# Second mixer of a two-layer fp32 network: TensorE order written out by hand, the sink as a column behind the keys, softmax scaling on GpSimd

## The chip, the cores and the metric

The program runs on one core of a Trainium2 chip. The metric is the device time of one execution in microseconds (us), the median over runs; times of the kernel before are shown below. Engines: TensorE (PE, matrix products), VectorE (DVE), ScalarE (ACT), GpSimd (POOL), SyncE (SP, which only issues DMA transfers here).

## The reference, cut to what matters

The network has two layers over 512 tokens of width 1024, all in fp32: mixer, feed-forward with a short convolution, gated embedding; the first layer's mixer is `mixer_ab`, the second layer's is `mixer_c`, which the change rewrites. It is attention in a sliding window with 16 query heads of 64 (4 key heads), blocks of 128 queries against 256 keys, and one learned "sink" per head: a logit that takes part in the softmax and has no value.

```python
q, k, v = jnp.split(h @ w_in, [1024, 1280], axis=-1)
q, k = rmsnorm(q heads, q_norm), rmsnorm(k heads, k_norm)
...
logits = einsum('bqhgd,bkhd->bhgqk', qn, kn) * 0.125 + bias
logits = where(mask, logits, -inf)
m = maximum(max(logits, -1), sink)
e = exp(logits - m)
w = e / (sum(e, -1) + exp(sink - m))
o = einsum('bhgqk,bkhd->bqhgd', w, vn)
...
h = h + o @ w_out
```

## The kernel before, in words

**Projections.** A product with fp32 accuracy is made of three: every operand is split into a high and a low half (fp32r), and `mm3` (L185 to L187) issues hi·hi, lo·hi, hi·lo. A projection tile (128 output rows x 512 tokens, buffer `psfm`) has 8 slices of the inner dimension, so 24 matmuls of 128x512, in two halves of 12. One half uses one weight chunk of 512 columns: `weights` (L157 to L172) loads it by DMA, ScalarE casts the high half (`whi`, L170), VectorE subtracts (`wlo`, L171). `fm_steps` yields after each half, and `fm` runs one to its end.

**The second mixer**, `mixer_c`. First come the keys' two projection tiles (a first stretch that starts as soon as input tiles are there), the values (`tm`, L218 to L220, buffer `pstm`), the token norms (`norm`, and `columns`, L270, buffer `psc`). Queries come in 8 tiles `jt` of two heads each. `project(jt)` is a projection with its scaling (`y`, L727) and its square (`sqc`, L729); `normed` sums squares per head with one fp32 matmul (`pn`, L735), ScalarE takes Ln and Exp (through the helper at L71), VectorE makes `qn` (L739).

The attention of a tile has two units of two blocks each (n0 = 0 and 2), 16 units in all:

- `scores(jt, n0)`: four fp32 matmuls on 64-row halves (`pl`, L765; 128 keys for block 0, else 256), four reductions on VectorE that add the bias and take the maximum with the sink (L771), the negated maximum `nm` and the sink's term `es` (L775, L776), four Exp on ScalarE in place in `lg`, which leave the sums in `dn`, one Exp of `es`, then `dn` plus `es` and its reciprocal (L783, L784), and four scalings of `lg` by it on VectorE (L788).
- `values(jt, n0)`: 6 or 8 transposes (`pt`, L800), copies out of PSUM (`wt`, ScalarE for one head, VectorE for the other, L806, L809), 6 or 8 matmuls with the values (`poc`, L817, on 64-column halves); after the second unit the tile is split for the output projection (L178, L179).

At the end `fill()` runs `embed`: the embedding projection of the next stage, 8 tiles of 6 matmuls (`pspp`), which need nothing of the mixer.

**What sets the order.** The program names the work of a tile in the order scores, projection, values of two units before; the Tile scheduler then orders every engine's instructions itself, so TensorE's queue may change from one kind of work to another after any matmul. Each engine executes its queue in order.

Of the kernel before, what the change touches and what calls it, by code (L numbers as in the profile page):

```python
# [23 lines left out]
NT = T // P  # L24
# [11 lines left out]
V_KN = V_QN + 1  # L36
# [9 lines left out]
PLAN = "hdsdhdsdhdsdhdhdshs"  # L46
LAST = "hdsdhdsdhdsdhdhshds"
SW_ORDER = [g * 4 + i for gg in (0, 2) for i in range(4) for g in (gg, gg + 1)]


class Kern:
# [649 lines left out]
    def mixer_c(self, st, bias, fill):  # L701
        nc, A = self.nc, self.A
        xs = st["xs"]
        W = A["w_c"]
        with ExitStack() as ctx:
            kp = self.pool("c_keep", 1, ctx=ctx)
            tp = self.pool("c_tmp", 2, ctx=ctx)
            first = self.lead([W[8], W[9]], st)
            pss = [t[:, a, :] for t in (self.zpair("pstm"), self.zpair("pstm")) for a in range(2)]
            tok = self.tm(A["w_cv"], xs, 256, pss)  # L710
            for _ in range(LEAD[0]):
                next(tok)
            self.norm(st, "hg")
            rstd = st["rstd"]
            for _ in range(LEAD[1]):
                next(tok)
            self.columns(st, "hg")
            sink = kp.tile([P, 16], F32, name="sink")
            nc.gpsimd.dma_start(out=sink, in_=A["sinks"].partition_broadcast(P))
            gq = kp.tile([P, 1], F32, name="gq")  # L720
            nc.vector.tensor_scalar(out=gq, in0=self.v(V_QN), scalar1=0.125, scalar2=None, op0=ALU.mult)

            def project(wi):

                ps = first.pop(0) if first else self.fm(W[wi], xs)
# [4 lines left out]
                return y, sq  # L730

# [9 lines left out]

            kn = [project(8 + i) for i in range(2)]
            kn = [normed(*x, self.v(V_KN), "kn", 2) for x in kn]
            vt = []
            for _ in tok:
                pass
            for i in range(NT):
                t = kp.tile([P, 256], F32, tag="vt", name="vt", bufs=4)
                nc.scalar.activation(t, pss[i][:, 0:256], AF.Identity, scale=st["rcol"][:, i:i + 1])
                vt.append(t)  # L750
            os_, qs, pos, pend = [], {}, {}, []

            def scores(jt, n0):

                q, kt = qs[jt], kn[jt // 4]
                wid = [128 if n == 0 else 256 for n in (n0, n0 + 1)]
                lg = []
                mx, nm, dn, es = [tp.tile([P, 4], F32, tag=t, name=t, bufs=4) for t in ("mx", "nm", "dn", "es")]
                pls = self.zpair("pl").rearrange("p a (i k) -> p a i k", i=2)
# [6 lines left out]
                for a in range(2):  # L766
                    hd = 2 * jt + a
                    l = tp.tile([P, 2, 256], F32, tag="lg", name="lg", bufs=6)
                    for i in range(2):
                        nk = wid[i]  # L770
# [3 lines left out]
                    lg.append(l)  # L774
                nc.vector.tensor_scalar(out=nm, in0=mx, scalar1=-1.0, scalar2=None, op0=ALU.mult)  # L775
                nc.vector.tensor_tensor(out=es.rearrange("p (a i) -> p a i", a=2), in0=nm.rearrange("p (a i) -> p a i", a=2),  # L776
                                        in1=sink[:, 2 * jt:2 * jt + 2].unsqueeze(2).broadcast_to([P, 2, 2]), op=ALU.add)
# [12 lines left out]

            def values(jt, n0, wid, lg):
                if n0 == 0:
                    pos[jt] = self.bank("poc", "hg")
                po = pos[jt]
                wts = []
                pts = self.zpair("pt").rearrange("p a (i k) -> p a i k", i=2)
                for a in range(2):
                    for i in range(2):
                        for b in range(wid[i] // P):
                            nc.tensor.transpose(out=pts[:, a, i, b * P:(b + 1) * P], in_=lg[a][:, i, b * P:(b + 1) * P], identity=self.ident)  # L800
                for a in range(2):
# [8 lines left out]
                    wts.append(wt)  # L810
                for i in range(2):
                    n = n0 + i
# [9 lines left out]

            two = [project(jt) for jt in range(2)]
            for jt in range(2):
                qs[jt] = normed(*two[jt], gq, "qn", 3)
            for jt in range(8):
                for n0 in (0, 2):
                    pend.append(scores(jt, n0))
                    if jt + 2 < 8:
                        if n0 == 0:  # L830
                            nxt = project(jt + 2)
                        else:
                            qs[jt + 2] = normed(*nxt, gq, "qn", 3)
                    if len(pend) > 2:
                        values(*pend.pop(0))
            for x in pend:
                values(*x)
            fill()
            return os_
# [46 lines left out]
    def embed(self, L, pp, pr):  # L886
# [3 lines left out]
        for c0 in range(2):  # L890
            for d0, hi, lo in self.weights(A[f"w_pp{L}"][c0], 1024):
                for j in range(2):
# [5 lines left out]
                    nc.scalar.copy(out=o, in_=ps)  # L898
                    pr.append(o)

    def ple(self, L, st, nxt, pp, pr):
        nc, A = self.nc, self.A
        xs = st["xs"]
        with ExitStack() as ctx:
            tp = self.pool(f"p_tmp{L}", 2, ctx=ctx)
            if pr:
                first = self.lead(A[f"w_pg{L}"][0:2], st)
            else:
                first = []
                self.embed(L, pp, pr)  # L910
            self.norm(st)
# [141 lines left out]
```

## Time and profile before

| what | value |
|---|---|
| median of 3 runs | 1327.49 us (1326.45 to 1328.64) |
| the profiled execution's own time | 1326.3 us |
| its span in the trace | 1324.5 us |
| TensorE busy | 1309.1 us, 99% of the span |
| VectorE, ScalarE, GpSimd busy | 65%, 52%, 1% |
| mean granted TensorE clock | 0.999 of full speed |

The profile shows one execution. The span runs from the first to the last instruction that the trace holds, and the execution's own time is 1.8 us longer. Busy shares are means over the whole program; the second mixer is about a tenth of it. In a row of the timeline, consecutive instructions of one form stand together with their count: one fp32 matmul (`pl`, `poc`, `pn`) is recorded as two, so that `pl ... x6` is three matmuls; a matmul of split halves (`psfm`) and a transpose are recorded as one. Durations of consecutive rows overlap by some tenths, because matmuls are pipelined; what a piece costs is the distance between the starts of two rows.

### The profile page before, as it was taken

How to read it: one execution, taken by the hardware profiler on the slowest of the kernel's cores; microseconds unless marked ns; L12 is line 12 of the kernel's file. 1: busy time of each engine (PE TensorE's matmuls, PEld its weight loads, DVE VectorE, ACT ScalarE, POOL GpSimd, SP SyncE). 2: the span in 40 equal slices, each digit the busy share in tenths (PEclk: the TensorE clock that was granted, in tenths of full speed). 3: DMA queues.
4: the chain of work that ended last, by engine and by line, in shares of the span. 5: the costliest groups of instructions: out<-in, count | busy, mean ns of one | idle time of the engine just before them, and what ended most of it. 6: DMA issues, size and time to landing. Idle time of an engine off the chain costs nothing.

```text
span 1324.5 us, 16856 instructions
## 1 busy us (share of the span) xinstructions
PE 1309.1 (99%) x6162; PEld 1055.2 (80%) x6162; DVE 863.1 (65%) x1609; ACT 684.0 (52%) x1224; POOL 18.7 (1%) x108
## 2 busy tenths in 40 slices
PE   9999999999999999999999999999999999999998
PEld 7787767788888888888888866678888888888887
DVE  6567876766677347776558387755777536776555
ACT  6566876845345224444465466654544324455341
POOL 2000000000000000000000000000000000000000
PEclk9999999999999999999999999999999999999999
DMA  6321211134553333323333211122332333332332
GB/s 208 108 64 49 59 39 47 48 98 116 90 142 98 106 102 101 99 91 94 107 112 91 85 48 32 33 82 94 102 102 89 94 107 96 96 96 88 90 109 80
DMA packets 38821, 118.96 MB, mean 90 GB/s; under 512 B 4433, under 2 KB 10881, under 8 KB 38737
## 3 DMA queue, kind: packets, MB, share of 16 engines
q1 hardware_dynamic: 38032, 116.41, 29.5%
q0 software_dynamic: 560, 1.45, 0.5%
q8 instruction: 48, 0.79, 0.2%
q14 instruction: 37, 0.30, 0.1%
q10 hardware_dynamic: 144, 0.02, 0.0%
HBM read 115.37 MB, written 2.49 MB: 89 GB/s over the span
## 4 chain that ended last, share of the span: by engine, by line
PE 93%; DVE 4%; ACT 2%; issue 1%; DMA 0%; SPq 0%; DVEq 0%; ACTq 0%
PE psfm L185 25%; PE psfm L187 25%; PE psfm L186 25%; PE pl L765 2%; PE poc L817 2%; PE pstm L220 1%; PE pstm L218 1%; PE pstm L219 1%; PE pt L800 1%; PE poa L593 1%; ACT sl L71 1%; PE psz L576 1%; PE pn L735 1%; PE psl L443 1%; PE pspp L185 1%; PE pspp L187 1%
## 5 line engine op out<-in xcount | busy, mean ns | idle before, releaser
L185 PE MATMUL psfm<-xhi,whi 128*128 128x512 f32 (+1 forms) x1200 | 470.8, 393 | 1.3 <-ACT xhi L235 1.3
L170 ACT CAST whi<-wraw 128x512 fp32r<-128x512 f32 (+1 forms) x428 | 260.0, 613 | 406.2 <-PE psfm L186 319.9
L186 PE MATMUL psfm<-xlo,whi 128*128 128x512 f32 (+1 forms) x1200 | 467.0, 389 | 0.8 <-DVE xlo L236 0.7
L187 PE MATMUL psfm<-xhi,wlo 128*128 128x512 f32 (+1 forms) x1200 | 467.5, 390 | 0.1
L171 DVE TENSOR_TENSOR wlo<-wraw,whi 128x512 fp32r<-128x512 f32 (+1 forms) x428 | 287.9, 677 | 170.4 <-ACT whi L170 149.5
L185 PEld LDWEIGHTS psfm<-xhi,whi 128*128 128x128 f32 x1200 | 226.0, 188 | 49.3 <-issue 2.0
L186 PEld LDWEIGHTS psfm<-xlo,whi 128*128 128x128 f32 x1200 | 225.8, 188 | 48.8 <-DVE xlo L236 2.3
L187 PEld LDWEIGHTS psfm<-xhi,wlo 128*128 128x128 f32 x1200 | 225.5, 188 | 47.6 <-issue 1.3
L185 PE MATMUL psfm<-ghi,whi 128*128 128x512 f32 x352 | 136.9, 389 | 0.0
L186 PE MATMUL psfm<-glo,whi 128*128 128x512 f32 x352 | 136.9, 389 | 0.0
L187 PE MATMUL psfm<-ghi,wlo 128*128 128x512 f32 x352 | 136.9, 389 | 0.0
L858 DVE TENSOR_TENSOR u<-psfm,rstd 128x512 f32<-128x512 f32 x88 | 60.7, 691 | 64.0 <-PE psfm L187 60.4
L861 ACT ACTIVATE cy<-u,vec 128x512 f32<-128x512 f32 x88 | 71.7, 817 | 43.8 <-DVE u L858 43.8
L862 DVE SCALAR_TENSOR_TENSOR cy<-u,vec,cy 128x512 f32<-128x512 f32 x88 | 66.1, 752 | 39.0 <-ACT cy L861 38.9
L185 PEld LDWEIGHTS psfm<-ghi,whi 128*128 128x128 f32 x352 | 66.1, 188 | 13.7
L187 PEld LDWEIGHTS psfm<-ghi,wlo 128*128 128x128 f32 x352 | 66.1, 188 | 13.7
L186 PEld LDWEIGHTS psfm<-glo,whi 128*128 128x128 f32 x352 | 66.1, 188 | 13.7
L291 DVE TENSOR_TENSOR h<-h,psfm 128x512 f32<-128x512 f32 x48 | 33.0, 688 | 57.3 <-PE psfm L187 57.3
L863 DVE SCALAR_TENSOR_TENSOR cy<-u,vec,cy 128x512 f32<-128x512 f32 x88 | 65.9, 751 | 2.7
L875 ACT CAST ghi<-cy 128x512 fp32r<-128x512 f32 x44 | 27.4, 623 | 49.4 <-DVE cy L872 49.4
L236 DVE SCALAR_TENSOR_TENSOR xlo<-h,gains,xhi 128x512 fp32r<-128x512 f32 x48 | 36.5, 761 | 7.0 <-ACT xhi L235 6.6
L235 ACT ACTIVATE xhi<-h,gains 128x512 fp32r<-128x512 f32 x48 | 34.6, 724 | 11.0 <-DVE h L291 6.8
(216 smaller groups left out, 1303.3 us busy)
## 6 DMA issues: line engine op xcount, KB each, us to landing
wraw<-w_up SPq DMA_DIRECT2D x88, 512.0 KB, 3.5
wraw<-w_dn SPq DMA_DIRECT2D x32, 512.0 KB, 3.5
wraw<-w_ab SPq DMA_DIRECT2D x18, 512.0 KB, 3.5
wraw<-w_pg SPq DMA_DIRECT2D x16, 512.0 KB, 3.5
wraw<-w_dn SPq DMA_DIRECT2D x32, 192.0 KB, 2.3
wraw<-w_c SPq DMA_DIRECT2D x10, 512.0 KB, 3.4
wraw<-w_abo SPq DMA_DIRECT2D x8, 512.0 KB, 3.6
wraw<-w_co SPq DMA_DIRECT2D x8, 512.0 KB, 3.5
```

The costliest lines, as they stand in the source:

```text
L170: nc.scalar.copy(out=hi[:, :d1 - d0], in_=r)
L171: nc.vector.tensor_tensor(out=lo[:, :d1 - d0], in0=r, in1=hi[:, :d1 - d0], op=ALU.subtract)
L185: t.matmul(ps, w[0], x[0], start=first, stop=False)
L186: t.matmul(ps, w[0], x[1], start=False, stop=False)
L187: t.matmul(ps, w[1], x[0], start=False, stop=last)
L235: nc.scalar.activation(hi, h, AF.Identity, scale=g)
L236: nc.vector.scalar_tensor_tensor(out=lo, in0=h, scalar=g, in1=hi, op0=ALU.mult, op1=ALU.subtract)
L291: self.nc.vector.tensor_tensor(out=self.h[m], in0=self.h[m], in1=ps, op=ALU.add)
L858: nc.vector.tensor_tensor(out=u[:, 2:], in0=ps, in1=rstd, op=ALU.mult)
L861: nc.scalar.activation(y, u[:, 2:], AF.Identity, scale=w[2], bias=w[3])
L862: nc.vector.scalar_tensor_tensor(out=y, in0=u[:, 1:T + 1], scalar=w[1], in1=y, op0=ALU.mult, op1=ALU.add)
L863: nc.vector.scalar_tensor_tensor(out=y, in0=u[:, 0:T], scalar=w[0], in1=y, op0=ALU.mult, op1=ALU.add)
```

## The change

1. In `mixer_c`, TensorE's instructions keep the order in which the program names them (`tc.manual_schedule` for that engine); the other engines are still ordered by the scheduler. The order is a table: before the scores of unit u stand DENSE[u] steps of `dense()`, where a step is half a projection (12 matmuls) for units 0 to 11 and a tile of the embedding projection (6 matmuls) after them. `embed` becomes a generator for that.
2. The transposes leave `values` and become `turned`. Behind the scores of unit u stand the value products of unit u-3, then (in even units) `pn` of the next query tile, then the transposes of unit u-2. From unit 14 on only one scored unit is kept back, from unit 16 on none, so that unit 14 turns two units.
3. The sink becomes column 256 of `lg`: GpSimd copies its negative there (L753 of the changed kernel), the reduction works on negated logits with a minimum, so that it gives `nm` itself, and the Exp runs over 129 or 257 columns, so that `dn` holds the sink's term. `mx`, `es`, its Exp and two small VectorE operations per unit go, the negation too.
4. The 64 scalings by `dn` go from VectorE to GpSimd (L771 of the changed kernel).

The matmuls are the same 5771 instructions in both programs.

```diff
+DENSE = [1] * 12 + [1, 2, 2, 1, 1, 1]
...
-                    l = tp.tile([P, 2, 256], F32, tag="lg", name="lg", bufs=6)
+                    nc.gpsimd.tensor_copy(out=lg[a][:, :, 256:257], in_=nsink[:, hd:hd + 1, :].broadcast_to([P, 2, 1]))
...
-                            out=l[:, i, :nk], in0=pls[:, a, i, :nk], in1=bias[:, hd, 256 - nk:256], scale=1.0,
-                            scalar=sink[:, hd:hd + 1], op0=ALU.add, op1=ALU.max, accum_out=mx[:, 2 * a + i:2 * a + i + 1])
+                            out=lg[a][:, i, 256 - nk:256], in0=pls[:, a, i, :nk], in1=bias[:, hd, 256 - nk:256], scale=-1.0,
+                            scalar=nsink[:, hd, :], op0=ALU.add, op1=ALU.min, accum_out=nm[:, c:c + 1])
-                nc.vector.tensor_scalar(out=nm, in0=mx, scalar1=-1.0, scalar2=None, op0=ALU.mult)
-                nc.vector.tensor_tensor(out=es.rearrange("p (a i) -> p a i", a=2), ...
...
-                        self.act(SET_EL, lg[a][:, i, :wid[i]], lg[a][:, i, :wid[i]], AF.Exp, bias=nm[:, c:c + 1], accum_out=dn[:, c:c + 1])
-                self.act(SET_EL, es, es, AF.Exp)
-                nc.vector.tensor_tensor(out=dn, in0=dn, in1=es, op=ALU.add)
+                        l = lg[a][:, i, 256 - wid[i]:257]
+                        self.act(SET_EL, l, l, AF.Exp, scale=-1.0, bias=nm[:, c:c + 1], accum_out=dn[:, c:c + 1])
                 nc.vector.reciprocal(out=dn, in_=dn)
...
-                        nc.vector.tensor_scalar(out=lg[a][:, i, :wid[i]], in0=lg[a][:, i, :wid[i]], scalar1=dn[:, c:c + 1], scalar2=None, op0=ALU.mult)
+                        nc.gpsimd.tensor_scalar(out=l, in0=l, scalar1=dn[:, c:c + 1], scalar2=None, op0=ALU.mult)
...
+                for u in range(18):
+                    for _ in range(DENSE[u]):
+                        next(d)
+                    if u < 16:
+                        scored.append(scores(u // 2, u % 2 * 2))
+                    for x in keyed:
+                        values(*x)
+                    keyed = []
+                    if u % 2 == 0 and u // 2 + 1 < 8:
+                        qs[u // 2 + 1] = normed(*got[u // 2 + 1], gq, "qn", 3)
+                    while len(scored) > (u < 14) + (u < 16):
+                        keyed.append(turned(*scored.pop(0)))
```

TensorE before, one tile `jt` in the middle of the mixer; a row is a line, an operation and a tile form, with a count where it repeats. Some single `psfm` rows stand between the pieces, and the other 21 or so of the tile follow in a row.

```order
L800 MATMUL pt<-cst,lg 128x128 x6
L765 MATMUL pl<-kn,qn 128x256
L817 MATMUL poc<-wt,vt 64x128
L765 MATMUL pl<-kn,qn 128x256 x2
L817 MATMUL poc<-wt,vt 64x128 x5
L765 MATMUL pl<-kn,qn 128x256
L735 MATMUL pn<-sqc,cst 128x512
L800 MATMUL pt<-cst,lg 128x128 x8
L185 MATMUL psfm<-xhi,whi 128x512
L765 MATMUL pl<-kn,qn 128x128 x2
```

```order
L765 MATMUL pl<-kn,qn 128x256
L817 MATMUL poc<-wt,vt 64x128
L765 MATMUL pl<-kn,qn 128x256
L186 MATMUL psfm<-xlo,whi 128x512
L817 MATMUL poc<-wt,vt 64x128 x7
L187 MATMUL psfm<-xhi,wlo 128x512
```

The two fences are one stretch, the second follows the first. The four score products of a unit stand in two or three pieces, with single value products between them.

TensorE after the change, in the same place: first an even unit (n0 = 0), with the last matmul of its 12 ahead of it, then an odd one.

```order
L189 MATMUL psfm<-xhi,wlo 128x512
L750 MATMUL pl<-kn,qn 128x128 x2
L750 MATMUL pl<-kn,qn 128x256 x2
L804 MATMUL poc<-wt,vt 64x128 x8
L729 MATMUL pn<-sqc,cst 128x512
L781 MATMUL pt<-cst,lg 128x128 x6
L187 MATMUL psfm<-xhi,whi 128x512
```

```order
L750 MATMUL pl<-kn,qn 128x256 x4
L804 MATMUL poc<-wt,vt 64x128 x6
L781 MATMUL pt<-cst,lg 128x128 x8
L187 MATMUL psfm<-xhi,whi 128x512
```

Score products, value products and transposes of a unit now stand each in one piece, and 12 `psfm` stand together between two units: a tile has 9 runs of one kind where it had 15.

GpSimd after the change, two units in the middle of the mixer, an odd one's scalings first (`dn` is the reciprocal sum, `nsink` the negated sink). Before, its queue held nothing in the mixer but the load of the sinks.

```order
L771 TENSOR_SCALAR lg<-lg,dn 128x256 x4
L753 COPY lg<-nsink 128x2
L771 TENSOR_SCALAR lg<-lg,dn 128x128
L771 TENSOR_SCALAR lg<-lg,dn 128x256
L771 TENSOR_SCALAR lg<-lg,dn 128x128
L771 TENSOR_SCALAR lg<-lg,dn 128x256
L753 COPY lg<-nsink 128x2 x3
```

One of an odd unit's two copies stands behind the four scalings of the unit before it, so that its third and fourth Exp wait for those.

## Rows read from the trace of the kernel before

**Rows 1.** Page, parts 1 and 2: busy times, and the granted clock in 40 slices.

```profile
PE 1309.1 (99%) x6162; PEld 1055.2 (80%) x6162; DVE 863.1 (65%) x1609; ACT 684.0 (52%) x1224; POOL 18.7 (1%) x108
...
PEclk9999999999999999999999999999999999999999
```

**Rows 2.** Timeline of PE, ends of the stretch: start us, us, instruction, [idle before].

```profile
736.98 0.95 PE L270 MATMUL psc<-cst,rstd 128*128 128x1 f32 x8
...
757.92 1.12 PE L735 MATMUL pn<-sqc,cst 128*128 128x512 f32 x2 [0.65 <-ACT sqc L729]
758.50 0.79 PE L185 MATMUL psfm<-xhi,whi 128*128 128x512 f32 x1
...
871.95 0.40 PE L185 MATMUL psfm<-xhi,whi 128*128 128x512 f32 x1
```

**Rows 3.** Timeline of PE, one query tile.

```profile
803.80 0.82 PE L800 MATMUL pt<-cst,lg 128*128 128x128 f32 x6
804.55 0.70 PE L765 MATMUL pl<-kn,qn 64*128 64x256 f32 x2
805.17 0.43 PE L817 MATMUL poc<-wt,vt 128*64 128x128 f32 x2
805.54 0.70 PE L765 MATMUL pl<-kn,qn 64*128 64x256 f32 x4
806.17 0.87 PE L817 MATMUL poc<-wt,vt 128*64 128x128 f32 x10
806.97 0.70 PE L765 MATMUL pl<-kn,qn 64*128 64x256 f32 x2
807.59 1.12 PE L735 MATMUL pn<-sqc,cst 128*128 128x512 f32 x2
808.56 1.04 PE L800 MATMUL pt<-cst,lg 128*128 128x128 f32 x8
809.35 0.47 PE L185 MATMUL psfm<-xhi,whi 128*128 128x512 f32 x1
809.75 0.92 PE L765 MATMUL pl<-kn,qn 64*128 64x128 f32 x6
810.63 0.43 PE L817 MATMUL poc<-wt,vt 128*64 128x128 f32 x2
...
812.05 1.09 PE L817 MATMUL poc<-wt,vt 128*64 128x128 f32 x14
813.07 0.50 PE L187 MATMUL psfm<-xhi,wlo 128*128 128x512 f32 x1
813.41 0.39 PE L185 MATMUL psfm<-xhi,whi 128*128 128x512 f32 x1
...
818.20 0.82 PE L800 MATMUL pt<-cst,lg 128*128 128x128 f32 x6
```

**Rows 4.** Timeline of PE, two units whose score products stand in one piece.

```profile
791.39 1.13 PE L765 MATMUL pl<-kn,qn 64*128 64x256 f32 x6
792.45 0.44 PE L817 MATMUL poc<-wt,vt 128*64 128x128 f32 x4
...
795.48 0.93 PE L765 MATMUL pl<-kn,qn 64*128 64x128 f32 x8
796.33 0.50 PE L185 MATMUL psfm<-xhi,whi 128*128 128x512 f32 x1
```

**Rows 5.** Windows: us, busy of PE, PEld, DVE, ACT, POOL, PEclk, DMA share, GB/s.

```profile
800.00:820.00 20.00, 20.00 (x121) 14.03 (x117) 14.66 (x53) 13.10 (x42) 0.00 (x0) 1.00 0.10 29
```

**Rows 6.** Groups by form, 775 to 872: count | busy us, mean ns | idle before.

```profile
L71 ACT ACTIVATE lg<-lg,nm 128x256 f32<-128x256 f32 x40 | 19.8, 497 | 0.0
L788 DVE TENSOR_SCALAR lg<-lg,dn 128x256 f32<-128x256 f32 x42 | 12.8, 348 | 0.0
```

**Rows 7.** Groups by form on POOL, whole span.

```profile
L312 POOL CAST hgm<-mf 128x384 uint8<-128x384 f32 x4 | 3.6, 932 | 0.7 <-DMA mf<-hgm 0.7
L148 POOL CAST cstr<-cstt 128x384 fp32r<-128x384 f32 x1 | 0.5, 510 | 0.6 <-DMA cstt<-cst 0.6
```

More of the change, by code (lines that the diff above doesn't have):

```diff
@@ L707, in mixer_c, with project @@
             tp = self.pool("c_tmp", 2, ctx=ctx)
[L708 to L717, printed above, removed]
             sink = kp.tile([P, 16], F32, name="sink")
             nc.gpsimd.dma_start(out=sink, in_=A["sinks"].partition_broadcast(P))
+            nsink = kp.tile([P, 16, 1], F32, name="nsink")
+            nc.vector.tensor_scalar(out=nsink[:, :, 0], in0=sink, scalar1=-1.0, scalar2=None, op0=ALU.mult)
             gq = kp.tile([P, 1], F32, name="gq")
             nc.vector.tensor_scalar(out=gq, in0=self.v(V_QN), scalar1=0.125, scalar2=None, op0=ALU.mult)
-            def project(wi):
-                ps = first.pop(0) if first else self.fm(W[wi], xs)
+            def project(wi, out):
+                ps = first.pop(0) if first else (yield from self.fm_steps(W[wi], xs))
                 y = tp.tile([P, T], F32, tag="y", name="y")
@@ L729, in project @@
                 nc.scalar.activation(sq, y, AF.Square)
-                return y, sq
+                out[wi] = (y, sq)
             def normed(y, sq, gain, tag, bufs):
@@ L740, in normed @@
                 return o
[L742 to L751, printed above, removed]
+            os_, qs, pos, got, kn, vt = [], {}, {}, {}, [None, None], []
             def scores(jt, n0):
@@ L756, in scores @@
                 wid = [128 if n == 0 else 256 for n in (n0, n0 + 1)]
-                lg = []
-                mx, nm, dn, es = [tp.tile([P, 4], F32, tag=t, name=t, bufs=4) for t in ("mx", "nm", "dn", "es")]
+                lg = [tp.tile([P, 2, 257], F32, tag="lg", name="lg", bufs=6) for _ in range(2)]
+                nm, dn = [tp.tile([P, 4], F32, tag=t, name=t, bufs=4) for t in ("nm", "dn")]
                 pls = self.zpair("pl").rearrange("p a (i k) -> p a i k", i=2)
@@ L767, in scores @@
                     hd = 2 * jt + a
[L768 removed]
+                    nc.gpsimd.tensor_copy(out=lg[a][:, :, 256:257], in_=nsink[:, hd:hd + 1, :].broadcast_to([P, 2, 1]))
+                for a in range(2):
+                    hd = 2 * jt + a
                     for i in range(2):
[L770 removed]
+                        nk, c = wid[i], 2 * a + i
                         nc.vector.tensor_tensor_reduce(
[L772 to L777 removed]
+                            out=lg[a][:, i, 256 - nk:256], in0=pls[:, a, i, :nk], in1=bias[:, hd, 256 - nk:256], scale=-1.0,
+                            scalar=nsink[:, hd, :], op0=ALU.add, op1=ALU.min, accum_out=nm[:, c:c + 1])
                 for a in range(2):
@@ L810, in values @@
                     wts.append(wt)
+                return jt, n0, wid, wts
+            def values(jt, n0, wid, wts):
+                if n0 == 0:
+                    pos[jt] = self.bank("poc", "hg")
+                po = pos[jt]
                 for i in range(2):
@@ L821, in values @@
                     os_.append(self.split_tile(self.xa, po))
[L823 to L835, printed above, removed]
@@ L836, in mixer_c, with dense @@
-            for x in pend:
-                values(*x)
-            fill()
+            def dense():
+                for jt in range(2, 8):
+                    steps = project(jt, got)
+                    next(steps)
+                    yield
+                    for _ in steps:
+                        pass
+                    yield
+                yield from fill()
+            first = self.lead([W[8], W[9]], st)
+            with tc.manual_schedule(engines={mybir.EngineType.PE}):
+                pss = [t[:, a, :] for t in (self.zpair("pstm"), self.zpair("pstm")) for a in range(2)]
+                tok = self.tm(A["w_cv"], xs, 256, pss)
+                for _ in range(LEAD[0]):
+                    next(tok)
+                self.norm(st, "hg")
+                rstd = st["rstd"]
+                for _ in range(LEAD[1]):
+                    next(tok)
+                self.columns(st, "hg")
+                for i in range(2):
+                    for _ in project(8 + i, got):
+                        pass
+                for _ in tok:
+                    pass
+                for i in range(NT):
+                    t = kp.tile([P, 256], F32, tag="vt", name="vt", bufs=4)
+                    nc.scalar.activation(t, pss[i][:, 0:256], AF.Identity, scale=st["rcol"][:, i:i + 1])
+                    vt.append(t)
+                for _ in project(0, got):
+                    pass
+                for i in range(2):
+                    kn[i] = normed(*got[8 + i], self.v(V_KN), "kn", 2)
+                for _ in project(1, got):
+                    pass
+                qs[0] = normed(*got[0], gq, "qn", 3)
+                d = dense()
+                scored, keyed = [], []
+                for u in range(18):
[10 more added lines that the diff above has]
+                        keyed.append(turned(*scored.pop(0)))
+                for x in keyed:
+                    values(*x)
+                for _ in d:
+                    pass
@@ L909, in ple @@
                 first = []
-                self.embed(L, pp, pr)
+                for _ in self.embed(L, pp, pr):
+                    pass
             self.norm(st)
```

11 lines of the change are left out of this document (5 added, 6 removed).

## The prediction

> **What bounds the kernel now.** I read the busy times first: TensorE is busy for 99% of the span, at a granted clock of nine tenths or more in each of the 40 slices [rows 1]. So time can leave only where TensorE does its work in less time, and the matmuls stay the same. What can shrink is what a matmul costs in its surroundings, and for that I went to TensorE's timeline in the mixer. The stretch that the change rewrites runs from the `psc` products at 736.98 to the first product of the output projection at 871.95: 134.97 us [rows 2]. The waits in it are small, 0.65 us ahead of the first `pn` being the largest [rows 2]. One query tile from transposes to transposes takes 818.20 − 803.80 = 14.40 us [rows 3].
>
> In that tile the reader is to see three prices, all as distances between starts:
> - 22 `psfm` from 813.07 to 818.20 take 5.13: the first .34, the other 21 take 4.79, so .228 each. A `psfm` alone between two other kinds costs .40 (809.35 to 809.75) [rows 3].
> - A lone score product (804.55, "x2") costs .62, and two together (805.54, "x4") .63: two products on the two 64-row halves run side by side, and one that stands alone pays for both [rows 3].
> - Value products likewise: one costs .37 (805.17), five .80 (806.17), seven 1.02 (812.05) [rows 3]. I take .80 for six (three pairs) and 1.02 for eight (four pairs).
>
> **The order of TensorE: the term that carries the sum.** Prices of the new pieces: 12 `psfm` are .40 + 11 × .228 = 2.91; 6 are 1.54. Four score products in one piece are .85 for an even unit (795.48 to 796.33) and 1.06 for an odd one (791.39 to 792.45, where three products fill the two pairs) [rows 4]. `pn` is .97, eight transposes .79 (808.56) [rows 3]; for six I take 6/8 of it, .59. So
> - even unit: 2.91 + .85 + 1.02 + .97 + .59 = 6.34;
> - odd unit: 2.91 + 1.06 + .80 + .79 = 5.56;
> - a tile 11.90 where it was 14.40, so 2.50 less.
>
> It can be checked from the other side. The odd unit's score products (804.55, 805.54, 806.97) cost .62 + .63 + .62 and the even one's .88 (809.75) and once more .62, in a piece like that at 804.55 which is left out [rows 3]; now 1.06 and .85: 1.46 less. Value products cost .37 + .80 + .37 + 1.02 [rows 3], now 1.82: .74 less. The rest is `psfm` that stood alone.
>
> The stretch, then: the opening (keys, values, first two query tiles) was 758.50 − 736.98 = 21.52; less the .65 of waiting, less one `pn` that moves back into unit 0 (.85, since part of it overlapped), plus .40 for one more change of kind: 20.4. Units 0 to 3: no value products before unit 3 and no transposes before unit 2, so 6.34 − 1.02 − .59 = 4.73, 5.56 − .80 − .79 = 3.97, 6.34 − 1.02 = 5.32, and 5.56, together 19.6. Units 4 to 11, four tiles, 47.6. Units 12 to 17 have one or two embedding tiles (1.54 or 2.91) in place of the projection: unit 12 is 4.97 and 13 is 5.56 by the same sums; 14, without `pn` but with two units' transposes, 2.91 + .85 + 1.02 + 1.38 = 6.16; 15, with 14 value products and six transposes, 5.01; the last two 1.54 + .80 + .79 and 1.54 + 1.02. Together 27.4. Sum 115.0.
>
> **The tail.** Nothing follows the last scored unit but embedding tiles, so here a wait may show. Between its score products and its transposes TensorE has 1.06 + 1.82 + .59 + 1.54 + .80 = 5.8 us of work. It needs a reduction, four Exp of .497 [rows 6] plus their sums, a reciprocal and four scalings: by these some 6 to 7. I take 1.0, with 0 and 3 as ends. Stretch 116.0, so 134.97 − 116.0 = **19.0 us** less.
>
> **Scaling on GpSimd.** Before, GpSimd does nothing in the mixer [rows 5], so no row has this operation there. Nearest rows: casts of 128x384 in .510 and .932 [rows 7]; by width a 128x256 lies between .34 and .62, and with no credit for the width .93 is the upper end. I take .45, as an fp32 result is nearer to the cheaper cast. 64 of them are 29 us of an engine that is otherwise idle; 8 per tile are 3.6 of 11.9. What hides them is the distance from a unit's scores to its transposes, two units or about 12 us, of which the chain up to the scaled `lg` needs 6 to 7. So their cost is nothing outside the tail, and a fall below nothing is excluded there, because TensorE is already without waits. Without that cover each unit would wait up to 1.8 us (4 × .45), 29 in all.
> A library load stands ahead of the first scaling, and no row shows its like. GpSimd is free from before 737, and the first transposes come some 33 us later (20.4 + 4.73 + 3.97 + 4.3), so it costs nothing up to about 30 us. The Trainium skill ("GPSIMD Engine Reference", section "2.1 Instruction dispatch") puts the first call of freshly loaded code at about 6 us; by that figure the sum stays as it is, and no row here shows it.
>
> **What this takes from the other engines.** VectorE was busy 14.66 of 20 us [rows 5], that is 10.6 per tile; eight scalings of at most .348 [rows 6] leave it, so 7.8 of the new 11.9. ScalarE, 13.10 of 20 [rows 5], has 9.4 per tile, less the Exp of `es`. Both fit, ScalarE with 2.5 us to spare. The small operations that the sink column removes (`nm`, `es`, its Exp, the addition) and the column that each Exp gains lie beside TensorE's work: nothing, covered by that same reserve; without it they would be worth about a microsecond per tile. The 32 copies of the sink go to GpSimd, between scalings. An odd unit's second copy stands behind four scalings of the unit before, and two of its Exp wait for it: those scalings end some 6.5 us after their score products, the Exp's turn comes some 9 after (one unit, then 3), so 2.5 us are left.
>
> **The sum.** The profiled execution took 1326.3; less 19.0 it is 1307.3. The median of the runs shown is 1.2 higher, 1327.49, and less 19.0 gives **1308.5**.
>
> **Rivals.**
> 1. *VectorE and ScalarE come late although their sums fit.* TensorE now follows a fixed order: when a reduction is late, the score products of the next unit stand still, and everything behind them too, where before another `psfm` could stand in the queue. For it: ScalarE's 9.4 of 11.9; VectorE and GpSimd work on the same buffers at once, which no row shows. If each of the three VectorE operations per tile with two inputs outside PSUM (`wlo` twice, `qn`) is held up by one scaling, that is 3 × .45 = 1.35 per tile, and if all of it reaches TensorE, 8 × 1.35 = 10.8: **1319.3**. The Trainium skill ("SBUF — State Buffer", "Who interferes with whom") states such a lock between a VectorE operation with two inputs in SBUF and a GpSimd operation that reads SBUF; no row here shows the two at work side by side. Against it: VectorE would still be at 9.2 of 11.9, and a unit has more than 5 us between the release of its scores and their reuse. Chance .12.
> 2. *The changes of kind were not what cost.* If single `psfm` cost the same in their new place, and only pairing returns: the lone score products of a tile (three, .31 each) and the lone value products (two, .18) give 1.3, so 8 × 1.3 = 10.4 less, **1317.1**. Against it: the same piece stands whole and split in the rows, .85 against 1.50. Chance .06.
> 3. *GpSimd becomes the bound* (slower). Its queue from the first scaling, about 29 us into the stretch, is 64 scalings of s, 32 copies of about .3 (an estimate, below the cheaper cast), and 4 us for the last transposes and values. The stretch is 29 + 64 s + 9.6 + 4: it decides from s = 1.15 on (116), and is as long as before at s = 1.45. At 2.0 it is 170.6, so 35.6 more: **1363**. For it: only two forms of GpSimd's work are in the trace, and twice the dearer of them is 1.9. Against it: both are below 1.15 at greater width. Chance .06.
> 4. *Waits in the tail and at the start eat the gain*, within .2% of before. Nothing points to 17 us of them. Chance .03.
>
> **How the numbers follow.** My forecast, chance .73, is 1305 (no wait in the tail, 2 us of overlaps that the distances hide) to 1313 (3 us in the tail, a few tenths of waiting in each unit). The likeliest is 1308.5. With a chance of .73 the range must take in another case; I take it to 1318, which covers rival 2 and most of rival 1, and leave out rivals 3 and 4 and the rest of 1. About .2%, 2.7 us, is what a measurement of this kernel can tell from no change. Faster by more: forecast, rivals 1 and 2, .91. Same: .03. Slower: rival 3, .06.
>
> **What would show it.** On the changed kernel's timeline of TensorE a tile in the middle should take 12.0 us within .3, in 9 runs, with score products of .85 and 1.06 and 12 `psfm` of 2.9; from `psc` to the output projection some 116 us; the wait ahead of the last transposes 0 to 3 us; scalings on GpSimd below 1 us each, VectorE about 8 of 12. Idle time of TensorE ahead of transposes released by GpSimd would speak for rival 3, ahead of score products by VectorE for rival 1, and full business with a longer tile for rival 2. The forecast is wrong if the stretch saves less than 12 us.

## The result, and the profile after

The changed kernel takes **1312.32 us** (median of 4 runs, 1311.30 to 1312.59) against 1327.28 before: a ratio of 0.9884, with a 95% interval from 0.9872 to 0.9897. That is 15.0 us less, where 19.0 were forecast; the forecast of 1308.5 was too low by 3.8, and the range from 1305 to 1318 holds the time. The profiled execution took 1311.3 us, with a span of 1309.5, so it stands 15.0 below the profiled execution of before too.

The page's busy times come first. They answer to [rows 1]:

```profile
PE 1293.6 (99%) x6162; PEld 1050.0 (80%) x6162; DVE 842.1 (64%) x1498; ACT 680.9 (52%) x1208; POOL 84.4 (6%) x204
```

TensorE executes the same 6162 recorded instructions in 15.5 us less of busy time. It is still busy for 99% of the span. GpSimd has 66 us more to do.

TensorE's timeline at the borders of the forecast's parts (start us, us, instruction, [idle before]), which answers to [rows 2]:

```profile
736.86 0.95 PE L272 MATMUL psc<-cst,rstd 128*128 128x1 f32 x8
...
750.77 1.12 PE L729 MATMUL pn<-sqc,cst 128*128 128x512 f32 x2 [0.78 <-ACT sqc L73]
752.67 0.50 PE L187 MATMUL psfm<-xhi,whi 128*128 128x512 f32 x1 [0.78 <-ACT sqc L73]
...
759.19 0.51 PE L187 MATMUL psfm<-xhi,whi 128*128 128x512 f32 x1
...
778.89 0.47 PE L187 MATMUL psfm<-xhi,whi 128*128 128x512 f32 x1
...
826.86 0.47 PE L187 MATMUL pspp<-whi 128*128 128x512 f32 x1
...
856.82 0.50 PE L187 MATMUL psfm<-xhi,whi 128*128 128x512 f32 x1
```

From the first to the last row the stretch is 119.96 us, where it was 134.97: the whole gain lies here. Its parts beside the forecast:

| part | forecast | measured | rows |
|---|---|---|---|
| opening, to the first projection of unit 0 | 20.4 | 22.3 | 736.86 to 759.19 |
| units 0 to 3 | 19.6 | 19.7 | to 778.89 |
| units 4 to 11, four tiles | 47.6 | 48.0 | to 826.86 |
| units 12 to 17 and the tail's wait | 27.4 + 1.0 | 30.0 | to 856.82 |
| sum | 116.0 | 120.0 | |

So the 4.0 us that are missing lie in the opening (1.9) and the tail (1.6), hardly in the tiles. One tile in the middle, on the same timeline; it answers to [rows 3]:

```profile
800.17 1.13 PE L750 MATMUL pl<-kn,qn 64*128 64x256 f32 x8
801.23 0.88 PE L804 MATMUL poc<-wt,vt 128*64 128x128 f32 x12
802.04 1.09 PE L781 MATMUL pt<-cst,lg 128*128 128x128 f32 x8
802.89 0.47 PE L187 MATMUL psfm<-xhi,whi 128*128 128x512 f32 x1
...
805.81 0.93 PE L750 MATMUL pl<-kn,qn 64*128 64x128 f32 x8
806.66 1.09 PE L804 MATMUL poc<-wt,vt 128*64 128x128 f32 x16
807.69 1.13 PE L729 MATMUL pn<-sqc,cst 128*128 128x512 f32 x2
808.65 0.82 PE L781 MATMUL pt<-cst,lg 128*128 128x128 f32 x6
...
812.15 1.14 PE L750 MATMUL pl<-kn,qn 64*128 64x256 f32 x8
```

The tile takes 812.15 − 800.17 = 11.98 us (14.40 before, 11.90 forecast), without a wait. Every piece has its forecast price within .06: score products 1.06 and .85, value products .81 and 1.03, `pn` .96, 12 `psfm` 2.92. Next, GpSimd's groups (count | busy us, mean ns of one | idle before):

```profile
L771 POOL TENSOR_SCALAR lg<-lg,dn 128x256 f32<-128x256 f32 x48 | 46.4, 979 | 9.8 <-DVE dn L766 9.8
L771 POOL TENSOR_SCALAR lg<-lg,dn 128x128 f32<-128x128 f32 x16 | 12.4, 776 | 40.7 <-DVE dn L766 40.6
```

A scaling of 128x256 takes .98 us on average. The forecast took .45, with .93 as the upper end [rows 7], so the average lies outside. In the same window form as [rows 5], 24 us or two tiles:

```profile
800.00:824.00 24.00, 24.00 (x170) 17.74 (x168) 16.05 (x54) 16.56 (x50) 16.85 (x25) 1.00 0.15 46
```

TensorE has no gap; per tile VectorE has 8.0, ScalarE 8.3 and GpSimd 8.4 of 12 us. Last the tail, on TensorE's timeline:

```profile
850.90 1.44 PE L804 MATMUL poc<-wt,vt 128*64 128x128 f32 x12
852.27 1.16 PE L781 MATMUL pt<-cst,lg 128*128 128x128 f32 x6
853.90 0.44 PE L781 MATMUL pt<-cst,lg 128*128 128x128 f32 x2 [0.46 <-POOL lg L771]
854.10 0.48 PE L187 MATMUL pspp<-whi 128*128 128x512 f32 x1
```

The last unit's transposes wait for its four scalings one by one: from 852.27 to 854.10 they take 1.83, where eight take .85 in the tile. The value products before them, those of the last unit but one, take 1.37 for .81, because their `wt` copies on ScalarE and VectorE come late. These two are 1.5 us.

### The profile page after: what moved, and what is told of

Read it like the earlier page. It is cut to its first block, busy times and chain, and to the rows that moved or that the text cites. A ratio compares the mean times of both kernels' runs of the same rounds, so it can differ in the third digit from the quotient of the medians.

```text
span 1309.5 us, 16936 instructions
## 1 busy us (share of the span) xinstructions
PE 1293.6 (99%) x6162; PEld 1050.0 (80%) x6162; DVE 842.1 (64%) x1498; ACT 680.9 (52%) x1208; POOL 84.4 (6%) x204
## 4 chain that ended last, share of the span: by engine, by line
PE 93%; DVE 3%; ACT 1%; POOL 1%; issue 1%; DMA 1%; SPq 0%; POOLq 0%; DVEq 0%; ACTq 0%
PE psfm L187 26%; PE psfm L188 26%; PE psfm L189 26%; PE pstm L220 1%; PE pstm L221 1%; PE pstm L222 1%; PE pl L750 1%; PE poa L595 1%; PE poc L804 1%; ACT sl L73 1%; POOL lg L771 1%; PE pn L729 1%; PE pt L781 1%; PE psz L578 1%; PE psl L445 1%
## 5 line engine op out<-in xcount | busy, mean ns | idle before, releaser
L188 PEld LDWEIGHTS psfm<-xlo,whi 128*128 128x128 f32 x1200 | 226.1, 188 | 46.4 <-DVE xlo L238 1.2
L884 POOL MEMSET u<- 128x2 f32 x88 | 8.6, 99 | 852.4 <-DVE cy L890 534.7
L771 POOL TENSOR_SCALAR lg<-lg,dn 128x128 f32<-128x128 f32 (+1 forms) x64 | 58.3, 928 | 50.5 <-DVE dn L766 50.4
```

Source lines behind the costliest of these rows:

```text
L188: t.matmul(ps, w[0], x[1], start=False, stop=False)
L771: nc.gpsimd.tensor_scalar(out=l, in0=l, scalar1=dn[:, c:c + 1], scalar2=None, op0=ALU.mult)
```

## The experiments

The theory was that the gain comes from TensorE's order (products in whole pieces, halves side by side, fewer changes of kind), and that the sink column and GpSimd's scaling lie beside it. Its rivals: the fixed order needs the other parts, or only changes of kind count, or only pairs do. Times of before, taken beside each group of runs, were 1327.0 (experiments 1 to 4), 1327.5 (5 to 7), 1327.1 (8 to 11) and 1327.6 (12). "The stretch" is always from `psc` to the first product of the output projection, 134.97 before and 119.96 after.

**1. The order alone.** TensorE's order of the change with the softmax of before.

```diff
-                lg = [tp.tile([P, 2, 257], F32, ...) for _ in range(2)]
+                mx, nm, dn, es = [...]
...
-                        nc.gpsimd.tensor_scalar(out=l, in0=l, scalar1=dn[:, c:c + 1], ...)
+                        nc.vector.tensor_scalar(out=lg[a][:, i, :wid[i]], ...)
```

> The TensorE order of the change alone: the softmax is that of the kernel before (maximum with the sink, es and its Exp, 64 scalings on VectorE). Theory (the gain is TensorE's order; the rest is beside it): a tile takes 12.0 us, VectorE is busy some 10.6 of it, and the tail gets shorter, since a scaling takes .35 on VectorE against .98 on GpSimd: 1310 to 1313 us. Rival (the fixed order needs the relieved VectorE): reductions come late, score products or transposes wait about half a us to 1 us per unit, 1318 to 1326 us.

Measured: 1320.96 us (1320.00 to 1321.53), ratio 0.9955 (0.9940 to 0.9969). The rival is right: the order alone gives 6.0 of the 15. TensorE's timeline, then VectorE's, around an odd unit:

```profile
803.90 1.13 PE L748 MATMUL pl<-kn,qn 64*128 64x256 f32 x8
804.96 0.43 PE L804 MATMUL poc<-wt,vt 128*64 128x128 f32 x2
806.01 0.98 PE L804 MATMUL poc<-wt,vt 128*64 128x128 f32 x10 [0.61 <-DVE wt L790]
```

```profile
803.89 0.16 DVE L766 TENSOR_TENSOR dn<-dn,es 128x4 f32<-128x4 f32 x1 [1.10 <-ACT es L73]
...
804.18 0.66 DVE L719 TENSOR_TENSOR y<-psfm,rstd 128x512 f32<-128x512 f32 x1
804.75 1.00 DVE L771 TENSOR_SCALAR lg<-lg,dn 128x128 f32<-128x128 f32 x4
805.67 0.62 DVE L790 COPY wt<-pt 128x128 f32<-128x128 f32 x2
```

The six value products take 1.96 (804.96 to the transposes at 806.92) and not .81, because their `wt` copy on VectorE stands in its queue behind the addition of `es`, which has waited 1.10 us for ScalarE's Exp, and behind four scalings. VectorE's sum fits the tile; its order does not.

**2. The rest alone.** Sink column and GpSimd's scaling in the kernel before, TensorE's order left to the scheduler.

```diff
-                        nc.vector.tensor_scalar(out=lg[a][:, i, :wid[i]], ...)
+                        nc.gpsimd.tensor_scalar(out=l, in0=l, ...)
```

> The other half: sink column and scaling on GpSimd, TensorE's order left to the scheduler as before. Theory: TensorE had next to no waits to remove, so nothing comes of it: 1326 to 1330 us, and a tile of 14.3 to 14.5 us. Rival (the softmax parts carry a share of the 15 us): 1323 us or less.

Measured: 1322.85 us (1322.50 to 1324.63), ratio 0.9972 (0.9960 to 0.9984): 4.1 less, against the theory. TensorE's waits were 1.5 us in the stretch and are 1.0 now, so next to none was there to remove. What differs is the order that the scheduler makes of the relieved engines:

```profile
803.38 0.82 PE L800 MATMUL pt<-cst,lg 128*128 128x128 f32 x6
...
809.25 0.93 PE L767 MATMUL pl<-kn,qn 64*128 64x128 f32 x8
...
817.53 0.81 PE L800 MATMUL pt<-cst,lg 128*128 128x128 f32 x6
```

The even unit's four score products now stand in one piece, where they were split in three and one [rows 3], and the tile takes 14.15. That and its like up to the fifth tile are 1.5 us; the other 2.5 lie behind it, where its timeline has 44 pieces for 54. So this is also a gain by TensorE's order, reached by another way. Which of the two parts gives it, no run separates.

**3. The change with its scaling on VectorE.**

```diff
-                        nc.gpsimd.tensor_scalar(out=l, in0=l, scalar1=dn[:, c:c + 1], ...)
+                        nc.vector.tensor_scalar(out=l, in0=l, scalar1=dn[:, c:c + 1], ...)
```

> The change with its 64 scalings on VectorE. Theory (GpSimd's .78 to .98 us per scaling is hidden between units but not behind the last ones): tiles stay at 12.0 us, the waits ahead of the last transposes and of the last value products shrink, 1 to 2.5 us less than the change: 1309.5 to 1311.5 us. Rival (VectorE needs the relief): 1314 us or more, with waits ahead of score products.

Measured: 1313.58 us (1313.09 to 1316.30), ratio 0.9907 (0.9890 to 0.9923), about 1.2 more than the change, which the intervals of the two ratios do not tell apart. Neither number was met: the tiles stay at 12.0, as the theory says, but the stretch is 122.2, 2.3 longer. Value products (2.0 us) and score products (.9) now wait for `wt` copies on VectorE, which also does the scalings: the shorter scalings take the last transposes back to .85, but the value products before them go from 1.37 to 2.16.

**4. Pairs apart.** The products of one head behind each other, in the same piece.

```diff
-                for i in range(2):
-                    ...
-                    for a in range(2):
+                for a in range(2):
+                    for i in range(2):
```

> The change, with the same products in the same pieces, but the two products of one 64-row or 64-column half behind each other instead of the two halves in turn (score and value products). Theory (two halves run side by side, and that is most of what the pieces give back): a piece of four score products goes from 1.06 to 1.7 or more, eight value products from 1.02 to 1.7 or more, some 2.5 to 3.5 us per tile, 8 tiles: 1332 to 1341 us. Rival (what cost was the change of kind, not the pairing): the pieces stay as they are, 1311 to 1314 us.

Measured: 1316.56 us (1315.94 to 1317.35), ratio 0.9923 (0.9908 to 0.9937): 4.2 above the change, between the two. On TensorE's timeline:

```profile
783.75 0.93 PE L750 MATMUL pl<-kn,qn 64*128 64x128 f32 x8
784.61 1.58 PE L804 MATMUL poc<-wt,vt 128*64 128x128 f32 x16
786.12 1.12 PE L729 MATMUL pn<-sqc,cst 128*128 128x512 f32 x2
```

Four score products cost what they did, .86; eight value products went from 1.02 to 1.51. The edit did not part what it was to part: with two score products per half, the second half's start beside the first half's all the same (.01 us behind them). With four value products per half they start .49 us behind, so they overlap only in part. Pairing had to be tested otherwise (experiment 6).

**5. Chains cut.** The same products, the projection's 12 in pieces of 3, 3 and 6: the piece behind the transposes joins that ahead of the next scores, so a unit has two more pieces, not the three of the expectation.

```diff
+                    if u < 12:
+                        next(d)
                     for x in keyed:
                         values(*x)
+                    if u < 12:
+                        next(d)
```

> The change, with each unit's 12 projection products cut in four pieces of 3: ahead of the score products, between them and the value products, between those and what follows, and behind the transposes. Score and value products stay whole. Theory (each change of kind costs by itself, about .17 us for the first projection product of a piece, and pieces keep a fixed cost at their ends): 3 more pieces in each of 12 units, some .17 each, 6 us: 1316 to 1320 us. Rival (only the products that stand alone cost, a change of kind is free): 1311.5 to 1313.5 us.

Measured: 1316.80 us (1315.57 to 1318.46), ratio 0.9923 (0.9909 to 0.9938). The time is in the theory's range. From its timeline, one tile:

```profile
796.07 0.93 PE L762 MATMUL pl<-kn,qn 64*128 64x128 f32 x8
...
808.59 0.71 PE L762 MATMUL pl<-kn,qn 64*128 64x128 f32 x6
```

The tile takes 12.52 us, .54 more than after for four more pieces: **.13 us for a change of kind**, here one to `psfm` and back, with all products kept. The trace also has one wait of 1.8 us for `qn` ahead of score products, so the 4 us are not all changes of kind.

**6. Halves apart.** Three projection products between the score products of the one head and those of the other.

```diff
-                    for a in range(2):
+                for a in range(2):
+                    if a and mid:
+                        next(d)
```

> The change, with 3 of the 12 projection products of units 0 to 11 moved in between the score products of the one head (one 64-row half) and those of the other. Theory (the halves run side by side only where both stand in one piece; in the run before, the records show the other half's products starting while the first half's were still at work): a piece of two products of one half costs what the four cost, 1.06 or .85, so an odd unit gains 1.06 and an even one .85, plus .2 for the projection's restart: 12 units, 13 to 14.5 us, 1325 to 1328 us. Rival (no running side by side, a piece costs .2 and each product its own share): 4 to 5 us, 1316 to 1318 us.

Measured: 1326.35 us (1325.38 to 1327.10), ratio 0.9994 (0.9984 to 1.0003), 14 above the change, as the theory had it. TensorE's timeline, an odd unit:

```profile
808.92 1.13 PE L764 MATMUL pl<-kn,qn 64*128 64x256 f32 x4
809.98 0.50 PE L187 MATMUL psfm<-xhi,whi 128*128 128x512 f32 x1
...
810.87 1.13 PE L764 MATMUL pl<-kn,qn 64*128 64x256 f32 x4
```

Two products of one half take 1.06 (808.92 to 809.98), as long as the four of both halves in one piece after the change. Two halves of the array do run side by side. The Trainium skill ("TensorEngine Tiling (Array Packing)", section "Key Properties") says that different tiles load weights and multiply in parallel; the 1.06 for two and for four agrees.

**7. Order and GpSimd's scaling, without the sink column.** As experiment 1, with

```diff
-                        nc.vector.tensor_scalar(out=lg[a][:, i, :wid[i]], ...)
+                        nc.gpsimd.tensor_scalar(out=lg[a][:, i, :wid[i]], ...)
```

> TensorE's order and the scaling on GpSimd, without the sink column (maximum, es and its Exp as before). Theory (in the run with the order alone, a wt copy on VectorE stood behind the sum's addition, which waits for the Exp of es, and four scalings; the scalings are .9 to 1.1 us of that delay): the wait ahead of an odd unit's value products falls from 1.2 to .1 to .4 us: 1313.5 to 1317 us. Rival (the wait for the Exp chain is what counts, the scalings are not): 1319 us or more.

Measured: 1319.60 us (1318.66 to 1320.35), ratio 0.9943 (0.9929 to 0.9958). The time is the rival's, the place is not: the odd unit's value products fell from 1.96 to 1.08 us, as the theory had it, and a tile takes 12.25 us, but from the scores of unit 12 to the output projection it takes 34.9 us, where the change takes 28.4. The end of it in the windows (us; busy time of PE, PEld, DVE, ACT, POOL; granted clock; DMA):

```profile
855.00:858.00 3.00, 1.05 (x14) 0.63 (x12) 0.55 (x3) 2.01 (x8) 0.86 (x1) 1.00 0.00 0
858.00:861.00 3.00, 1.96 (x7) 0.93 (x8) 0.00 (x0) 0.00 (x0) 2.77 (x4) 0.68 0.00 0
861.00:866.00 5.00, 5.00 (x25) 3.63 (x24) 2.75 (x4) 2.82 (x5) 0.00 (x0) 0.51 0.01 3
```

TensorE stands still for half of 855 to 861, behind a chain that ends with the last scalings. Its granted clock is .68 in the second window and .51 in the third, so that the last embedding tile and the last value products run at the lower level, 1.2 GHz: they take 2.84 and 1.90 us, where the change takes 1.56 and 1.16. These 2.0 us are the clock's and not the chain's.

**8. The change once more**, as the base of the next three.

> The change once more, on the chip of the next three: 1311.5 to 1313 us.

Measured: 1312.48 us (1311.27 to 1312.76), ratio 0.9891 (0.9877 to 0.9906).

**9. The keys' norms apart.**

```diff
-                for _ in project(0, got):
-                    pass
-                for i in range(2):
-                    kn[i] = normed(*got[8 + i], self.v(V_KN), "kn", 2)
-                for _ in project(1, got):
-                    pass
+                for jt in range(2):
+                    steps = project(jt, got)
+                    next(steps)
+                    kn[jt] = normed(*got[8 + jt], self.v(V_KN), "kn", 2)
+                    for _ in steps:
+                        pass
```

> The change, with the two pn products of the keys a projection tile apart (one inside that of query tile 0, one inside that of tile 1) and not behind each other. Theory (the second pn and the projection behind it wait .78 us each for ScalarE's Ln of the one before, since they use its bank): 1.4 to 2 us less than the change, 1310.3 to 1311 us. Rival (the waits only move to the next norm): within .4 us of the change.

Measured: 1310.47 us (1309.68 to 1311.23), ratio 0.9878 (0.9862 to 0.9895): 2.0 less than experiment 8. From `psc` to the first projection of unit 0 it now takes 20.3 us, and both waits of .78 are gone. The theory holds, and the forecast's 20.4 for the opening with it.

**10. An embedding tile later.**

```diff
-DENSE = [1] * 12 + [1, 2, 2, 1, 1, 1]
+DENSE = [1] * 12 + [1, 1, 2, 1, 2, 1]
```

> The change with one of the embedding tiles of unit 13 moved to unit 16 (table end 1, 1, 2, 1, 2, 1), so that the last scalings on GpSimd have 1.4 us more of TensorE's work beside them. Theory (ahead of the last value products and transposes TensorE waits .57 and .97 us): 1 to 1.5 us less than the change, 1310.8 to 1311.5 us. Rival (unit 14, which turns two units, then waits as much more): within .4 us of the change.

Measured: 1310.48 us (1309.90 to 1311.70), ratio 0.9879 (0.9865 to 0.9894): 2.0 less by the medians. In the traces units 12 to 17 take 28.8 us for 30.0, so 1.2 of it is shown to be the tail.

**11. Both edits.**

> Both of these edits: if both theories hold, 2.4 to 3.5 us less than the change, 1308.8 to 1310 us, which is what the forecast took for opening and tail.

Measured: **1309.38 us** (1308.57 to 1309.53), ratio 0.9868 (0.9854 to 0.9883), 3.1 less than the change and the best kernel of this study. Its stretch is 117.0 us. The value products of the last unit but one are back at .81, and the last eight transposes are down from 1.83 to 1.10.

**12. GpSimd's share doubled.**

```diff
                         nc.gpsimd.tensor_scalar(out=l, in0=l, scalar1=dn[:, c:c + 1], ...)
+                        nc.gpsimd.tensor_scalar(out=l, in0=l, scalar1=1.0, ...)
```

> The change, with a second GpSimd operation (a product with 1) behind each of the 64 scalings, so that GpSimd's share doubles: some 7 times .92 plus .60 per tile becomes twice that, 14 to 15 of 12.0 us. Theory (GpSimd's queue then is the bound, from about 1.15 us per scaling on): the stretch is 29.7 us to the first scaling, 64 x 1.8, the 32 copies at .2, and 4 us for the last transposes and values, 155 us in place of 120: 1343 to 1350 us, and TensorE waits for GpSimd at the transposes of every unit. Rival (the two units between scores and transposes hide it as well): 1314 to 1318 us, waits in the tail alone.

Measured: 1342.57 us (1341.79 to 1342.77), ratio 1.0114 (1.0097 to 1.0131): slower than before, .4 us below the range of the theory. The two largest waits of TensorE in the stretch (instruction, releaser: us in total, times, longest):

```profile
PE poc L805 <- ACT wt L788: 9.6, 3, 3.7
PE pt L782 <- POOL lg L772: 7.6, 10, 2.2
```

GpSimd's groups in that run:

```profile
L771 POOL TENSOR_SCALAR lg<-lg,dn 128x256 f32<-128x256 f32 x48 | 46.5, 974 | 7.0 <-DVE dn L766 7.0
L772 POOL TENSOR_SCALAR lg<-lg 128x256 f32<-128x256 f32 x48 | 41.9, 882 | 0.0
```

With 9.6 and 8.7 for the two forms of 128x128 that is 106.7 us, 1.67 for each of the 64. From its first scaling to its last GpSimd is busy for 108.6 of 115.7 us: it is the bound. TensorE's waits are 20 us in all, 2 in the change, while the stretch is 29.5 longer; in four parts of it, 17.1 us together, the granted clock was .50, and how much that adds no run separates. Part of the waiting shows at the value products: their `wt` copies on ScalarE stand behind Exp that wait for a sink copy in GpSimd's queue. That is an explanation from the queues, which no run of its own tests.

## Why the prediction was right, and where it was off

**The order of TensorE** was priced right. The tile fell from 14.40 to 11.98 where 11.90 were forecast. By kind, score products went from 3.37 [rows 3] to 1.91, value products from 2.56 to 1.84, and the rest (transposes, lone `psfm`) gave .2, as the forecast had it. What causes it is shown by experiment 6 (two halves side by side: 14 us when the score products' halves are parted in 12 units) and 5 (.13 for a change of kind to `psfm` and back). How the 2.42 us divide is an estimate: rival 2 priced the lost pairing at 1.3, and 1.1 more came, .18 for each of the six pieces that went. Most of these were changes between score and value products, which no run prices by themselves.

**The step that failed** is that what the sink column removes is worth "nothing, covered by that same reserve". Over TensorE's new order it is worth 7.4 us with the scaling on VectorE (1320.96 to 1313.58) and 6.7 with it on GpSimd (experiments 7 and 8, 7.9 and 14.6 under the kernel before beside them). The forecast's own price without the reserve, about a microsecond per tile, is near both. It counted busy time per tile: 7.8 on VectorE, where 8.0 are measured, and 9.4 on ScalarE, read from 20 us that are no whole number of tiles, where 8.3 are measured. Both fit, but these operations stand in a chain. Without the column one `nm` is made from all four maxima, so the first Exp waits for the last reduction; with it each reduction leaves its own `nm`. An odd unit's first reduction on VectorE and its first Exp on ScalarE, in experiment 1:

```profile
806.20 0.48 DVE L754 CUSTOM_DVE_ANT_0 lg<-pl,bias,sink 128x256 f32<-128x256 f32 x1
...
808.62 0.51 ACT L73 ACTIVATE lg<-lg,nm 128x256 f32<-128x256 f32 x1
```

The same two after the change:

```profile
813.47 0.48 DVE L758 CUSTOM_DVE_ANT_0 lg<-pl,bias,nsink 128x256 f32<-128x256 f32 x1
...
814.05 0.51 ACT L73 ACTIVATE lg<-lg,nm 128x257 f32<-128x257 f32 x1 [0.43 <-DVE nm L758]
```

From the one to the other it is 2.42 us, and .58 after the change; from the start of the score products to the reciprocal it is 7.1 and 4.0. VectorE's wait for the last Exp is not the difference, since its reciprocal waits 1.0 us for it in the change too. But the later chain puts this wait and the scalings ahead of the `wt` copies for which TensorE stands still. This is read from the traces; no run changes `nm` alone. With the scaling on VectorE most of the loss lies in the tiles (units 4 to 11 take 52.6 us in experiment 1 and 48.0 in 3). With it on GpSimd nearly all lies in units 12 to 17 (36.5 in experiment 7, 30.0 in the change), where little work hides the longer chain (for the last unit 6.8 us from score products to reciprocal, 4.0 in the change), and 2.0 of that is the clock. Rival 1 named such lateness, but put it at the score products and priced it by the lock. The change escapes it because it has the sink column, not because VectorE's sum fits. The total came out because the change holds both parts: order alone 6.0, the rest alone 4.1, both 15.0.

**The opening** was forecast at 20.4 "less the .65 of waiting". That wait went and two of .78 came: the program order puts the two `pn` of the keys behind each other, and the second, and the projection behind it, wait for ScalarE to be done with the one before. Experiment 9 takes them away, and 20.3 are measured.

**GpSimd's scaling** was mis-sized: .98 and .78 on average against .45, and .92 and .60 where nothing holds it up, with .93 as the upper end that the casts gave. The step on its cover held none the less, since the tiles have no wait. By the medians, moving the scaling there is worth 1.2 us (experiments 3 and 8, 13.4 and 14.6 under the kernel before beside them) to 1.8 (1 and 7, 6.0 and 7.9), less than the intervals tell apart; in the traces the stretch is 2.3 and 1.3 us shorter. It comes from clearing VectorE's queue, in spite of the scaling's own time. Rival 3's point of decision, 1.15 us per scaling, was near: the change spends .92 (46.4 + 12.4 over 64). With the 106.7 us of experiment 12 its formula gives 29 + 106.7 + 9.6 + 4 = 149.3 us, and the stretch of that run is 149.5. So close is in part luck: the formula puts 9.6 for copies, which took 6.5, and leaves out the 7.1 that GpSimd waited between its first scaling and its last.

**The tail** was forecast with 1.0 of waiting, from 0 to 3; it is 2.6 over the sum of its pieces, 1.5 of it at the last transposes (1.0) and at the value products before them (.6). For the transposes the size of the scaling is why: four take 3.6 us and not 1.8. The value products wait for their `wt` copies, which the forecast did not count. Experiment 10 confirms the place.

**The library load** cost nothing that shows: before its first scaling GpSimd waits 39 us for `dn`, and that scaling takes .61, as later ones of its form do. How long the load takes, no run here shows.

## What to carry to other kernels

When TensorE is busy 99% of the time, look at what a product costs by what stands beside it: a lone product on half the array cost as much as two here, and a change of kind .13 us. Before an order is fixed by hand, follow the chains through the in-order queues of the other engines: a small operation that must wait for all of several others holds back everything behind it, so shares of busy time do not tell whether it fits. Price an operation that moves to an unused engine with a wide range, and know the point at which it becomes the bound.

## What was not expected of the hardware

**GpSimd and VectorE hold each other up.** GpSimd's timeline after the change, each scaling by itself, two of either form, and then VectorE's at the same time, with a third operation from a later unit:

```profile
805.53 0.93 POOL L771 TENSOR_SCALAR lg<-lg,dn 128x256 f32<-128x256 f32 x1
806.43 1.39 POOL L771 TENSOR_SCALAR lg<-lg,dn 128x256 f32<-128x256 f32 x1
809.57 0.60 POOL L771 TENSOR_SCALAR lg<-lg,dn 128x128 f32<-128x128 f32 x1
811.05 1.13 POOL L771 TENSOR_SCALAR lg<-lg,dn 128x128 f32<-128x128 f32 x1
```

```profile
806.34 0.69 DVE L173 TENSOR_TENSOR wlo<-wraw,whi 128x512 fp32r<-128x512 f32 x1 [0.82 <-ACT whi L172]
811.03 0.75 DVE L733 SCALAR_TENSOR_TENSOR qn<-y,gq,sqc 128x512 f32<-128x512 f32 x1 [0.58 <-ACT sqc L73]
...
818.33 0.93 DVE L173 TENSOR_TENSOR wlo<-wraw,whi 128x512 fp32r<-128x512 f32 x1 [1.00 <-ACT whi L172]
```

A scaling that starts just behind `wlo` or `qn` takes about .5 us longer than its like, while those keep their usual .69 and .75. The second `wlo` starts .09 us behind a scaling (818.24) and takes .93 itself. The Trainium skill ("SBUF — State Buffer", section "Who interferes with whom") says that a VectorE operation with two inputs in SBUF and a GpSimd operation that reads SBUF exclude each other, and that the one issued first goes first. The trace agrees that they hold each other up, and on the order too but for one scaling, which starts .06 us ahead of a `wlo` and still loses .5. But the loss is not alike: four `wlo` that start .09 to .24 us behind a scaling lose .09 to .25, and those that start .28 us or more behind lose nothing, though a scaling runs for .60 or .92. Beside `xlo`, which has one input in PSUM, neither gets longer (the scaling at 809.57). In the whole stretch the scalings lose 5.4 us and VectorE .8, so here it was mostly GpSimd that waited, not VectorE as rival 1 had it, and the two units of cover hid it.

**The order within a piece matters little** for four products on two halves (experiment 4: .86 either way), more for eight value products (1.51 against 1.02).

**The clock** fell to its lower level in experiment 7 (.68 and .51) when TensorE had stood still for half of 855 to 861, and in experiment 12 in four places (.50), each behind a wait of TensorE, so that waits there cost more than their own length.
